# A hybrid attention and state-space layer on one core: joint softmax of two key heads, the scan's state part inside the output's accumulation, and a wider output projection

## The chip, the cores and the metric

The kernel runs on one core of a Trainium2 chip. A core has five engines with instruction queues of their own: TensorE (PE; its weight loads are listed as PEld), VectorE (DVE), ScalarE (ACT), GpSimd (POOL) and SyncE (SP), which here issues all DMAs. Matmuls write PSUM, which has eight banks of 128 partitions by 512 float32; all else lies in SBUF. The metric is the device time of one execution in microseconds, the median of several runs.

## The reference, cut to what matters

One layer is computed for a prompt of 2048 tokens and for a sample group of 8 sequences of 8 tokens. An input projection feeds an attention branch and a state-space branch (SSD), gates weigh both, and an output projection adds the result to the input:

```python
def sink_attention(q, k, v, mask, sinks):            # 16 heads, 4 key heads, window 128
    s = where(mask, einsum(q, k) * HEAD_DIM ** -0.5, -inf)
    m = maximum(s.max(-1), sink);  p = exp(s - m)
    p = p / (p.sum(-1) + exp(sink - m));  return einsum(p, v)

def ssd_scan(x, dt, A, Bm, Cm, h0, chunk):           # 32 heads in 4 groups, chunk 128, state 128
    a_cs = cumsum(dt * A)                            # inside a chunk
    y_diag = einsum(C @ B, exp(a_cs_l - a_cs_s) causal, dt * x)
    states = einsum(Bm, exp(a_cs_end - a_cs) * dt, x)
    h_next = h * exp(a_cs_end) + states              # from chunk to chunk
    y_off  = einsum(Cs, h_prev, exp(a_cs))           # the state's part of the output
    return y_diag + y_off

merged = sigmoid(g_a) * (o_a * silu(z_a)) @ w_attn_proj + sigmoid(g_s) * o_s @ w_ssd_proj
y = x + merged @ w_out                               # 1024 x 1024
```

All inputs and results are float32. The large products split both operands into a high and a low part of a reduced format (`F32R`) and add three products (`SPLIT3`), so a projection over 1024 input channels is 8 x 3 = 24 matmuls.

## The kernel before, in words

The prompt is cut into 4 blocks of 512 tokens, each into 4 tiles (or chunks) of 128. Three phases follow one another. Phase T1 projects and does attention, phase S projects and does the scan, phase T2 does both branch projections, the gates, the merge and the output projection, with the sample group's attention and scan among the first block of T2. The program is written in this order, and a scheduler, which simulates a timeline, sets the order of each engine's queue; there it places attention and scan work among the projections' matmuls. Each queue then runs strictly in its order. Buffers come from pools with a fixed number per tag; who takes one that is still read waits.

**T1, attention.** `attn_unit` handles a pair of key heads and one token tile, 32 units in all. For each key head (four query heads) it makes scores `sc` in PSUM (L541), brings them to `s` (ACT copy L547, masked DVE copy L548), takes the row maximum (L553) and calls `softmax` (L378 to L393): five small DVE operations on 128 x 4, five ACT exponentials, then two of the four heads scaled by ACT (L391) and two by POOL (L393). `s` is then transposed by TensorE (L558), spread into two masked halves `PT` (L560), and when both key heads are there, multiplied with the values (L570).

**S, scan.** For each of 4 groups (8 heads) and 4 chunks, 64 chunks in all, 60 with a state to start from, `AB` is loaded with the cumulated decay of 8 heads on all partitions (L884), `L` is made of it (ACT L887, L888, POOL L889), and `py` is the product of `L` and `dx` (L910): 8 float32 matmuls with 64 stationary columns, which write the upper and the lower half of the partitions in turn. The trace shows every float32 matmul as two passes, each with its own weight load. The state's part is made apart: two DMAs load the decay once more as `EB` (L894), ACT takes its exponential (L895), four matmuls of 128 stationary columns multiply the state `H` with `CT` into `po`, a PSUM bank of its own (L898), and DVE multiplies `po` with `EB` (L899). DVE adds `py` to the skip term `u` (L926), and POOL adds `EB` (L928). `H` is renewed from `st` (L916) by DVE (L923). `py` has one bank.

**T2, output projection.** For each block, four times: 256 channels of `w_o` are loaded (1 MB) and split (ACT L150, DVE L151), and for each of 4 token tiles (in one block a fifth of 64 sample rows) 24 matmuls of 128 x 256 (L210) fill half a PSUM bank. DVE adds the input `xr` into `y` (L1316), which is stored. `xr` and `y` have two buffers each.

Of the kernel before, what the change touches and what calls it, by code (L numbers as in the profile page):

```python
# [17 lines left out]
P = 128  # L18
D = 1024
KT = D // P  # L20
TB = 512
# [57 lines left out]
def build(tc, nc, a, o, seq, phases=("T1", "S", "T2"), dbg=None):  # L79
# [298 lines left out]
    def softmax(wk, s, mx, width, nsk, sk, n):  # L378
        ng = wk.tile([P, 4], F32, name="ng", tag="ng")
        V.scalar_tensor_tensor(out=ng[:, :n], in0=mx[:, :n], scalar=-1.0, in1=nsk, op0=ALU.mult, op1=ALU.min)  # L380
        es_ = wk.tile([P, 4], F32, name="es", tag="es")
        V.tensor_tensor(es_[:, :n], sk, ng[:, :n], ALU.add)
        A.activation(es_[:, :n], es_[:, :n], AF.Exp)
        den = wk.tile([P, 4], F32, name="den", tag="den")
        for i in range(n):
            A.activation(s[:, i, :width], s[:, i, :width], AF.Exp, bias=ng[:, i : i + 1], accum_out=den[:, i : i + 1])  # L386
        V.tensor_tensor(den[:, :n], den[:, :n], es_[:, :n], ALU.add)
        V.tensor_scalar(den[:, :n], den[:, :n], 2.0, None, ALU.mult)
        V.reciprocal(den[:, :n], den[:, :n])  # L389
        for i in range(min(n, 2)):  # L390
            A.activation(s[:, i, :width], s[:, i, :width], AF.Copy, scale=den[:, i : i + 1])  # L391
        for i in range(2, n):
            G.tensor_scalar(s[:, i, :width], s[:, i, :width], den[:, i : i + 1], None, ALU.mult)  # L393

    def phase_t1():
        with ExitStack() as es:
# [12 lines left out]
            sp = pool("sp", 5)  # L409
# [69 lines left out]
            def v_tile(b, hT):  # L479
# [6 lines left out]
                dtt = wk.tile([P, NT, 32], F32, name="dtt", tag="dtt", bufs=1)  # L486
# [40 lines left out]
            def attn_unit(b, pair, tt, qTs, zs):  # L527
# [3 lines left out]
                PTs = []  # L531
                po = trp.tile([P, HG, P], F32, name="tr", tag="tr")
                for kvl in range(2):
                    kv = 2 * pair + kvl
                    s = sp.tile([P, HG, P], F32, name="s", tag="s")
                    mx = smp.tile([P, HG], F32, name="mx", tag="mx")
                    for hh in range(2):
                        sc = scp.tile([P, 2, 256], F32, name="sc", tag="sc")
                        for h in range(2):
                            for i in range(2):  # L540
                                PE.matmul(  # L541
                                    sc[:, h, :W], qTs[kvl][:, 2 * hh + h], KTT[:, i, kv, k0 : k0 + W],
                                    start=i == 0, stop=i == 1,
                                )
                        if full:
                            sv = s[:, 2 * hh : 2 * hh + 2]
                            A.copy(sv, sc[:, :, P:])  # L547
                            V.copy_predicated(sv, older.unsqueeze(1).to_broadcast([P, 2, P]), sc[:, :, :P])  # L548
                        else:
                            for h in range(2):  # L550
                                masked_max(s, mx, 2 * hh + h, sc[:, h, :P], mask, P)
                    if full:
                        V.tensor_reduce(mx, s, AX.X, ALU.max)  # L553
                    softmax(smp, s, mx, P, nsink[:, 4 * kv : 4 * kv + 4], sink[:, 4 * kv : 4 * kv + 4], HG)
                    PT = ptp.tile([P, 2, HG, P], F32, name="PT", tag="PT")
                    tr = trp.tile([P, HG, P], F32, name="tr", tag="tr")
                    for hg in range(HG):
                        PE.transpose(tr[:, hg], s[:, hg], ident)  # L558
# [191 lines left out]
    def phase_s():  # L750
        with ExitStack() as es:
# [14 lines left out]
            yp = pool("y2", 1, space=PSUM)  # L766
            yop = pool("yo2", 1, space=PSUM)
# [99 lines left out]
            def ssd_group(b, g, xT, BT, CT, zs, dt, acs, dec, wd):  # L867
# [11 lines left out]
                for c in range(NT):  # L879
# [47 lines left out]
                    if not first:  # L927
                        G.tensor_tensor(u, u, EB, ALU.add)  # L928
# [246 lines left out]
    def phase_t2():  # L1175
        w_a, w_s, w_o = a["w_attn_proj"][0], a["w_ssd_proj"][0], a["w_out"][0]
        wav = w_a.rearrange("(q v h d) c -> v d q h c", q=2, v=2, h=HG)
        with ExitStack() as es:
# [29 lines left out]

            def wa_load(j):
# [27 lines left out]

            order = [NB - 1] + list(range(NB - 1))
# [9 lines left out]
            for b in order:  # L1248
# [5 lines left out]
                for kh in range(2):  # L1254
# [7 lines left out]
                    if b == order[0] and kh == 1:  # L1262
                        phase_sa(oas)
                        phase_ss(vss)
                    for j in range(4):
# [35 lines left out]
                for j in range(4):  # L1301
                    cs = slice(256 * j, 256 * j + 256)
                    _, hl = wload([(0, w_o[:, cs])])
                    for tt in range(NT + smp):
                        n = P if tt < NT else 64
                        ps = mm()
                        proj_tm(ps[:n, :256], hl, 256, mg, tt, n)
# [5 lines left out]
                        x = wk.tile([P, 256], F32, name="xr", tag="xr")  # L1313
                        SY.dma_start(x[:n], src)
                        y = wk.tile([P, 256], F32, name="y", tag="y")
                        V.tensor_tensor(y[:n], ps[:n, :256], x[:n], ALU.add)  # L1316
                        SY.dma_start(dst, y[:n])
# [47 lines left out]
```

## Time and profile before

| | us |
|---|---|
| median of 3 runs (3144.47 to 3152.12) | 3145.01 |
| the profiled execution | 3143.59 |
| its span, first to last instruction | 3141.8 |
| T1, about 0 to 741 | 741.0 |
| S, about 741 to 1950 | 1209.0 |
| T2 to the last output projection, to 3092 | 1142.0 |
| the last block's output projection, from 3092 | 49.8 |

The phases overlap somewhat at their borders. A row of the profile names a line, an engine, an operation and its tiles as output<-input, then how often it stands there. Busy times of matmuls include their way through the array, which overlaps with the next one's, so that the pace of TensorE is better read from a long piece of the chain divided by its count than from a mean duration. The mean granted clock of TensorE over the span was 0.992.

### The profile page before, as it was taken

To read this page: it belongs to the slowest core of one execution; us is meant where nothing else is said; L and a number is where in the kernel's file an instruction comes from. 1 tells how busy PE (TensorE), PEld (TensorE's weight loads), DVE (VectorE), ACT (ScalarE), POOL (GpSimd) and SP (SyncE) were. 2 spreads that over 40 slices of the span, in tenths; PEclk is the share of its full clock that TensorE was granted. 3 is DMA by queue.
4 is the path that set the end of the run, shared out by engine and by line. 5 is a ranking of instruction groups with operands and counts; after the bars stand their busy time and mean duration, and the time that the engine had idled before them with its cause. 6 is when DMAs were issued, how large, how long until landed. Compare 5 with 4: busy or idle time off the path is not lost.

```text
span 3141.8 us, 49127 instructions
## 1 busy us (share of the span) xinstructions
PE 3059.9 (97%) x18982; PEld 2635.5 (84%) x18982; DVE 1918.5 (61%) x3142; ACT 1356.5 (43%) x2863; POOL 933.1 (30%) x925
## 2 busy tenths in 40 slices
PE   8999999998999999999999998999999999999999
PEld 7979797976999888778877877878878899999888
DVE  5868767677666666676666665456556644333433
ACT  4656545455555444444445453343333322222321
POOL 2425232432455444555554554100111110000000
PEclk9999999999999999999999998999999999999999
DMA  6635345254777755665666564455655663345443
GB/s 223 189 106 148 112 120 166 68 185 154 243 256 259 282 207 202 233 228 188 222 244 212 201 219 142 149 141 172 208 176 144 177 193 123 103 147 159 138 107 104
DMA packets 409986, 553.72 MB, mean 176 GB/s; under 512 B 34145, under 2 KB 347257, under 8 KB 399497
## 3 DMA queue, kind: packets, MB, share of 16 engines
q1 hardware_dynamic: 409752, 550.59, 54.1%
q8 instruction: 149, 2.44, 0.3%
q14 instruction: 85, 0.69, 0.1%
HBM read 445.31 MB, written 107.30 MB: 176 GB/s over the span
## 4 chain that ended last, share of the span: by engine, by line
PE 78%; DVE 8%; DMA 4%; POOL 4%; issue 3%; ACT 2%; SPq 0%; POOLq 0%; DVEq 0%; ACTq 0%
PE mm L199 49%; PE mm L210 13%; PE mm L186 6%; DVE acc L792 2%; PE tr L570 2%; PE sc L541 2%; DVE whl L151 1%; PE py L910 1%; POOL ws L913 1%; POOL L L889 1%; PE tr L558 1%; PE st L916 1%; PE po L898 1%; DMA v<-v_d 1%; DVE zs L929 1%
## 5 line engine op out<-in xcount | busy, mean ns | idle before, releaser
L199 PE MATMUL mm<-hT,whl 128*128 128x512 f32 (+1 forms) x6720 | 1341.4, 355 | 6.1 <-DVE whl L151 3.0
L199 PEld LDWEIGHTS mm<-hT,whl 128*128 128x128 f32 x6720 | 1117.5, 189 | 175.8 <-issue 7.4
L199 PE MATMUL mm<-ot,whl 128*128 128x512 f32 (+1 forms) x2880 | 567.9, 354 | 3.0 <-DVE whl L151 1.4
L199 PEld LDWEIGHTS mm<-ot,whl 128*128 128x128 f32 x2880 | 474.9, 188 | 74.0 <-DVE whl L151 2.9
L151 DVE TENSOR_TENSOR whl<-raw,whl 128x2048 fp32r<-128x2048 f32 (+1 forms) x172 | 366.7, 2137 | 266.5 <-ACT whl L150 259.4
L150 ACT CAST whl<-raw 128x2048 fp32r<-128x2048 f32 (+1 forms) x172 | 298.4, 1746 | 218.0 <-PE mm L199 101.2
L210 PE MATMUL mm<-whl,hT 128*128 128x256 f32 (+1 forms) x2304 | 303.5, 286 | 2.7 <-DVE dtt L491 2.2
L210 PEld LDWEIGHTS mm<-whl,hT 128*128 128x128 f32 x2304 | 286.8, 189 | 7.9 <-issue 4.1
L792 DVE SCALAR_TENSOR_TENSOR acc<-cr,cwb,acc 128x512 f32<-128x512 f32 x288 | 272.5, 948 | 27.3 <-ACT acc L787 24.9
L889 POOL TENSOR_TENSOR L<-L,cbm 128x1024 f32<-128x1024 f32 x64 | 162.2, 2546 | 146.5 <-DVE cbm L878 139.5
L210 PE MATMUL mm<-whl,ot 128*128 128x256 f32 (+1 forms) x1632 | 204.0, 284 | 0.0
L210 PEld LDWEIGHTS mm<-whl,ot 128*128 128x128 f32 (+1 forms) x1632 | 198.8, 188 | 3.7 <-issue 2.1
L186 PE MATMUL mm<-hT,whl 128*128 128x512 f32 x768 | 192.7, 400 | 2.2 <-ACT hT L295 2.1
L887 ACT ACTIVATE L<-AB,acs 128x128 f32<-128x128 f32 x512 | 157.5, 390 | 63.1 <-PE py L910 29.3
L186 PEld LDWEIGHTS mm<-hT,whl 128*128 128x128 f32 x768 | 141.2, 190 | 33.5 <-ACT hT L295 2.5
L859 DVE SCALAR_TENSOR_TENSOR zs<-th,mm 128x512 f32<-128x512 f32 (+1 forms) x80 | 45.6, 577 | 152.4 <-ACT th L858 151.9
L393 POOL TENSOR_SCALAR s<-s,den 128x128 f32<-128x128 f32 x128 | 79.3, 632 | 198.7 <-DVE den L389 144.1
L858 ACT ACTIVATE th<-mm 128x512 f32<-128x512 f32 (+1 forms) x80 | 40.0, 508 | 202.8 <-PE mm L199 196.7
L150 ACT CAST ot<-v 128x512 fp32r<-128x512 f32 x96 | 58.7, 620 | 159.5 <-DVE v L1231 81.0
L386 ACT ACTIVATE s<-s,ng 128x128 f32<-128x128 f32 x256 | 99.9, 394 | 39.9 <-DVE ng L380 32.6
L1231 DVE SCALAR_TENSOR_TENSOR v<-v,snw,rb 128x512 f32<-128x512 f32 x64 | 49.3, 786 | 97.6 <-DMA v<-v_d 97.4
L913 POOL TENSOR_TENSOR ws<-wx,ws 128x512 fp32r<-128x512 f32 x64 | 106.4, 1663 | 5.1 <-ACT ws L912 4.9
(324 smaller groups left out, 3899.6 us busy)
## 6 DMA issues: line engine op xcount, KB each, us to landing
raw<-in_w_in_dram SPq DMA_DIRECT2D x72, 1024.0 KB
whl<-w_dx SPq DMA_DIRECT2D x24, 2048.0 KB
whl<-w_dz SPq DMA_DIRECT2D x24, 2048.0 KB
hT<-h_d SPq DMA_DIRECT2D x80, 512.0 KB
AB<-ac_d SPq DMA_DIRECT2D x64, 512.0 KB
raw<-in_w_ssd_proj_dram SPq DMA_DIRECT2D x32, 1024.0 KB
whl<-w_dbc SPq DMA_DIRECT2D x12, 2048.0 KB
raw<-in_w_in_dram SPq DMA_DIRECT2D x40, 512.0 KB
```

The costliest lines, as they stand in the source:

```text
L150: A.copy(hi, src)
L151: V.tensor_tensor(lo, src, hi.bitcast(F32), ALU.subtract)
L186: PE.matmul(ps, hl[:, x, k, c0 : c0 + P], ht[:, y, :], start=first and i == 0, stop=last and i == n - 1,)
L199: PE.matmul(ps, hl[:, x, k, c0 : c0 + P], ht[:, y, lo : lo + n], start=i == 0, stop=i == 3 * len(hT) - 1,)
L210: PE.matmul(ps, ht[:, x, tt * P : tt * P + m], hl[:, y, k, :n], start=i == 0, stop=i == 3 * len(hT) - 1,)
L386: A.activation(s[:, i, :width], s[:, i, :width], AF.Exp, bias=ng[:, i : i + 1], accum_out=den[:, i : i + 1])
L393: G.tensor_scalar(s[:, i, :width], s[:, i, :width], den[:, i : i + 1], None, ALU.mult)
L541: PE.matmul(sc[:, h, :W], qTs[kvl][:, 2 * hh + h], KTT[:, i, kv, k0 : k0 + W], start=i == 0, stop=i == 1,)
L792: V.scalar_tensor_tensor(out=acc, in0=raw[:, k : k + TB], scalar=cwb[:, k, ct : ct + 1], in1=acc, op0=ALU.mult, op1=ALU.add)
L887: A.activation(L[:, h], AB[:, h], AF.Relu, scale=-1.0, bias=acs[:, hc.start + h : hc.start + h + 1])
L889: G.tensor_tensor(L, L, cbm[:, c].unsqueeze(1).to_broadcast([P, 8, P]), ALU.mult)
L913: G.tensor_tensor(ws[:, 1], wx, ws[:, 0].bitcast(F32), ALU.subtract)
```

## The change

Three edits. Softmax is done once for both key heads of a unit, on 8 columns, after the scores of both; ACT then scales the first key head's four rows, POOL the second's. In the scan, `AB` itself is raised to the exponential after `L` has been made and multiplied by `CT` on DVE, so that the state's part is a second product into the same PSUM tile `py`, which now has two banks; `EB`, its DMAs, `po` and two additions are gone. The output projection takes 512 channels at a time and half of the input channels: four (or five) PSUM banks stay open over both halves.

```diff
     def softmax(wk, s, mx, width, nsk, sk, n):
-        for i in range(min(n, 2)):
+        for i in range((n + 1) // 2):
             A.activation(s[:, i, :width], s[:, i, :width], AF.Copy, scale=den[:, i : i + 1])
-        for i in range(2, n):
+        for i in range((n + 1) // 2, n):
             G.tensor_scalar(s[:, i, :width], s[:, i, :width], den[:, i : i + 1], None, ALU.mult)
...
-            sp = pool("sp", 5)
+            sp = pool("sp", 3)
...
+                s = sp.tile([P, 2 * HG, P], F32, name="s", tag="s")
+                mx = smp.tile([P, 2 * HG], F32, name="mx", tag="mx")
                 for kvl in range(2):
...
-                    if full:
-                        V.tensor_reduce(mx, s, AX.X, ALU.max)
-                    softmax(smp, s, mx, P, nsink[:, 4 * kv : 4 * kv + 4], sink[:, 4 * kv : 4 * kv + 4], HG)
+                if full:
+                    V.tensor_reduce(mx, s, AX.X, ALU.max)
+                heads = slice(2 * HG * pair, 2 * HG * pair + 2 * HG)
+                softmax(smp, s, mx, P, nsink[:, heads], sink[:, heads], 2 * HG)
+                PTs = []
+                for kvl in range(2):
...
-            yp = pool("y2", 1, space=PSUM)
-            yop = pool("yo2", 1, space=PSUM)
+            yp = pool("y2", 2, space=PSUM)
...
                     if not first:
-                        EB = lp.tile([P, 4, P], F32, name="EB", tag="EB")
-                        for hl in range(2):
-                            src = ac_d[b][hc].rearrange("(i l) t -> l i t", l=2)[hl]
-                            SY.dma_start(EB[64 * hl : 64 * hl + 64], src.partition_broadcast(64))
-                        A.activation(EB, EB, AF.Exp)
-                        po = yop.tile([P, 4, P], F32, name="po", tag="po")
-                        for i in range(4):
-                            PE.matmul(po[:, i], H[g][:, i * P : (i + 1) * P], CT[:, sl], start=True, stop=True)
-                        V.tensor_tensor(EB, po, EB, ALU.mult)
+                        A.activation(AB, AB, AF.Exp)
+                        V.tensor_tensor(AB, AB, CT[:, sl].unsqueeze(1).to_broadcast([P, 8, P]), ALU.mult)
...
                     for i in range(4):
-                        for hl in range(2):
-                            PE.matmul(py[64 * hl : 64 * hl + 64, i], dx[:, 2 * i + hl], L[:, 2 * i + hl], start=True, stop=True)
-                    ws = ck.tile([P, 2, 8, 64], F32R, name="ws", tag="ws", bufs=1)
+                        for src, mov in ((dx, L), (H[g].rearrange("p (h d) -> p h d", h=8), AB))[: 1 if first else 2]:
+                            for hl in range(2):
+                                PE.matmul(
+                                    py[64 * hl : 64 * hl + 64, i], src[:, 2 * i + hl], mov[:, 2 * i + hl],
+                                    start=src is dx, stop=first or src is not dx,
+                                )
+                    ws = ck.tile([P, 2, 8, 64], F32R, name="ws", tag="ws")
...
-                    if not first:
-                        G.tensor_tensor(u, u, EB, ALU.add)
...
-                for j in range(4):
-                    cs = slice(256 * j, 256 * j + 256)
-                    _, hl = wload([(0, w_o[:, cs])])
-                    for tt in range(NT + smp):
-                        ps = mm()
-                        proj_tm(ps[:n, :256], hl, 256, mg, tt, n)
+                for j in range(2):
+                    cs = slice(512 * j, 512 * j + 512)
+                    pss = [mm() for tt in range(NT)]
+                    if smp:
+                        pss.append(extra["mm"].tile([P, TB], F32, name="mms", tag="mms")[:64])
+                    for kh in range(2):
+                        hl = wide_load(w_o[512 * kh : 512 * kh + 512, cs])
+                        for tt, ps in enumerate(pss):
+                            for i in range(12):
+                                kk, (x, y) = i // 3, SPLIT3[i % 3]
+                                PE.matmul(
+                                    ps, mg[4 * kh + kk][:, x, tt * P : tt * P + ps.shape[0]], hl[:, y, kk],
+                                    start=kh == 0 and i == 0, stop=kh == 1 and i == 11,
+                                )
...
-                        V.tensor_tensor(y[:n], ps[:n, :256], x[:n], ALU.add)
-                        SY.dma_start(dst, y[:n])
+                        x = wk.tile([P, TB], F32, name="xr", tag="xr")
+                        SY.dma_start(x[:n], src)
+                        V.tensor_tensor(x[:n], ps, x[:n], ALU.add)
+                        SY.dma_start(dst, x[:n])
```

(`wide_load` loads 1 MB as 4 x 128 input channels by 512 output channels and splits it like `wload`. A small tile `dtt` of T1 now shares the buffer of `zt`.)

Three places show how the queues move. The first is TensorE in the scan, two chunks of the last group of a block, as it stood before:

```order
L199 MATMUL mm<-hT,whl 128x512 x8
L910 MATMUL py<-L,dx 64x128 x7
L898 MATMUL po<-CT,H_8560 128x128 x4
L910 MATMUL py<-L,dx 64x128
L916 MATMUL st<-ws,Bt 128x512
L199 MATMUL mm<-hT,whl 128x512 x22
L916 MATMUL st<-ws,Bt 128x512 x2
L199 MATMUL mm<-hT,whl 128x512 x9
L910 MATMUL py<-L,dx 64x128 x8
```
The same place now, where `AB` is the decayed `CT`, `H_8175` the same state as `H_8560`, and L906 and L915 are what L910 and L916 were:

```order
L915 MATMUL st<-ws,Bt 128x512
L906 MATMUL py<-L,dx 64x128 x2
L915 MATMUL st<-ws,Bt 128x512 x2
L897 MATMUL tr<-cst,xT 128x128 x4
L199 MATMUL mm<-hT,whl 128x512 x3
L897 MATMUL tr<-cst,xT 128x128 x4
L199 MATMUL mm<-hT,whl 128x512 x9
L906 MATMUL py<-AB,H_8175 64x128 x2
L906 MATMUL py<-L,dx 64x128 x2
```
The four wide matmuls of the state are gone from between the `py` products. In their place two of 64 columns follow each two of `dx`, on to four such pairs, so every `py` run after the first two matmuls needs the renewed `H`; 97 runs of `py` have become 105, of up to 16 matmuls instead of 8.

The second is ACT at the end of T1, in the last attention units, as it stood before (L386 is an exponential with its sum `den`, L391 the scaling, L547 the copy of scores):

```order
L386 ACTIVATE s,den<-s,ng 128x128 x4
L391 ACTIVATE s<-s,den 128x128 x2
L383 ACTIVATE es<-es 128x4
L391 ACTIVATE s<-s,den 128x128 x2
L386 ACTIVATE s,den<-s,ng 128x128 x4
L547 COPY s<-sc 128x256
L391 ACTIVATE s<-s,den 128x128 x2
L386 ACTIVATE s,den<-s,ng 128x128 x3
L383 ACTIVATE es<-es 128x4
```
The same place now, under the same lines:

```order
L391 ACTIVATE s<-s,den 128x128 x4
L547 COPY s<-sc 128x256 x3
L386 ACTIVATE s,den<-s,ng 128x128 x8
L547 COPY s<-sc 128x256
L383 ACTIVATE es<-es 128x8
L386 ACTIVATE s,den<-s,ng 128x128 x2
L391 ACTIVATE s<-s,den 128x128 x4
L383 ACTIVATE es<-es 128x8
```
Runs of four exponentials with a scaling of two each have become runs of eight with a scaling of four, so the first scaling of a unit stands behind the exponentials of both key heads.

The third is DVE in the last output projection, as it stood before:

```order
L151 TENSOR_TENSOR whl<-raw,whl 128x2048
L1297 SCALAR_TENSOR_TENSOR ot<-ac,ot 128x512
L1316 TENSOR_TENSOR y<-mm,xr 128x256 x4
L151 TENSOR_TENSOR whl<-raw,whl 128x2048
L1316 TENSOR_TENSOR y<-mm,xr 128x256 x4
L151 TENSOR_TENSOR whl<-raw,whl 128x2048
L1316 TENSOR_TENSOR y<-mm,xr 128x256 x8
```
The same place now, where L1331 is the addition of the input, and L1301 and L1304 were L1294 and L1297:

```order
L1301 TENSOR_TENSOR ac<-ac,t 128x512
L151 TENSOR_TENSOR whl<-raw,whl 128x2048
L1304 SCALAR_TENSOR_TENSOR ot<-ac,ot 128x512
L151 TENSOR_TENSOR whl<-raw,whl 128x2048
L1331 TENSOR_TENSOR xr<-mm,xr 128x512 x4
L151 TENSOR_TENSOR whl<-raw,whl 128x2048
L1331 TENSOR_TENSOR xr<-mm,xr 128x512 x4
```
Sixteen additions of 256 channels have become eight of 512, in two groups of four; the last weight split (L151) stands between the groups, behind four additions that each need their input's DMA.

## Rows read from the trace of the kernel before

**Rows 1.** The page, parts 1 and 4: busy time by engine; chain by engine.
```profile
PE 3059.9 (97%) x18982; PEld 2635.5 (84%) x18982; DVE 1918.5 (61%) x3142; ACT 1356.5 (43%) x2863; POOL 933.1 (30%) x925
PE 78%; DVE 8%; DMA 4%; POOL 4%; issue 3%; ACT 2%; SPq 0%; POOLq 0%; DVEq 0%; ACTq 0%
```

**Rows 2.** Four stretches of the program; stretch, its length, busy us (instructions) by engine.
```profile
0.00:741.00 741.00, 698.63 (x4847) 595.78 (x4847) 529.10 (x1105) 399.70 (x1144) 247.54 (x312) 0.99 0.45 142
741.00:1950.00 1209.00, 1181.47 (x6993) 1001.98 (x6991) 817.53 (x1101) 587.62 (x1197) 608.73 (x531) 0.99 0.64 223
2586.00:3092.00 506.00, 505.31 (x3167) 467.23 (x3168) 201.72 (x230) 140.69 (x176) 0.00 (x0) 1.00 0.43 130
3092.00:3141.80 49.80, 46.53 (x387) 46.25 (x385) 15.38 (x22) 6.24 (x4) 0.00 (x0) 1.00 0.32 101
```

**Rows 3.** The chain of waits, longest pieces; start us, length us, what.
```profile
2816.67 57.00 PE mm L210 x480
2907.71 184.75 PE mm L199 x813
3092.46 46.08 PE mm L210 x384
```

**Rows 4.** Groups by line and shape; after the bar: busy us, mean ns.
```profile
L210 PE MATMUL mm<-whl,ot 128*64 128x256 f32 x96 | 11.6, 276 | 0.0
L1294 DVE TENSOR_TENSOR ac<-ac,t 128x512 f32<-128x512 f32 x24 | 16.6, 691 | 0.7
L1316 DVE TENSOR_TENSOR y<-mm,xr 128x256 f32<-128x256 f32 x64 | 26.3, 421 | 75.4 <-PE mm L210 41.1 <-DMA xr<-in_x_prompt_dram 31.4 <-PE st L1129 2.8
```

**Rows 5.** Instructions in order of time, end of the program; start us, length us.
```profile
3113.17 0.42 DVE L1316 TENSOR_TENSOR y<-mm,xr 128x256 f32<-128x256 f32 x1 [2.97 <-DMA xr<-in_x_prompt_dram]
3138.57 0.42 DVE L1316 TENSOR_TENSOR y<-mm,xr 128x256 f32<-128x256 f32 x1 [2.45 <-PE mm L210]
```

**Rows 6.** Groups by line and shape in the scan stage.
```profile
L910 PE MATMUL py<-L,dx 128*64 128x128 f32 x1024 | 81.3, 282 | 5.0 <-DVE xT L926 5.0
L910 PEld LDWEIGHTS py<-L,dx 128*64 128x64 f32 x1024 | 58.0, 137 | 31.1 <-issue 23.9 <-DVE EB L899 1.8 <-DVE zs L929 1.4
L898 PE MATMUL po<-CT,H 128*128 128x128 f32 x480 | 67.3, 284 | 5.0 <-DVE H L923 5.0
L898 PEld LDWEIGHTS po<-CT,H 128*128 128x128 f32 x480 | 60.7, 195 | 11.6 <-DVE H L923 7.1 <-issue 2.6 <-DVE BT L797 0.7
L928 POOL TENSOR_TENSOR xT<-xT,EB 128x512 f32<-128x512 f32 x60 | 87.2, 1454 | 47.6 <-DVE xT L926 27.1 <-DVE EB L899 20.4
L560 DVE TENSOR_TENSOR PT<-tr,halves 128x1024 f32<-128x1024 f32 x60 | 72.3, 1216 | 22.3 <-PE tr L558 22.1
```

**Rows 7.** Instructions in order of time, one chunk of the scan, weight loads.
```profile
1930.15 1.08 PEld L898 LDWEIGHTS po<-CT,H 128*128 128x128 f32 x8
1931.35 0.85 PEld L910 LDWEIGHTS py<-L,dx 128*64 128x64 f32 x16
1932.38 0.19 PEld L916 LDWEIGHTS st<-ws,Bt 128*128 128x128 f32 x1 [0.17 <-issue]
```

**Rows 8.** Waits of TensorE and its weight loads; us in total, times, longest.
```profile
PEld po L898 <- DVE H L923: 7.1, 6, 2.8
PE py L910 <- DVE xT L926: 5.0, 5, 1.3
PE tr L558 <- ACT s L391: 5.0, 3, 2.6
```

**Rows 9.** Groups by line and shape in the softmax.
```profile
L387 DVE TENSOR_TENSOR den<-den,es 128x4 f32<-128x4 f32 x64 | 11.5, 182 | 34.7 <-ACT s L386 34.4
L553 DVE TENSOR_REDUCE mx<-s 128x4 f32<-128x512 f32 x60 | 40.8, 679 | 0.5
L386 ACT ACTIVATE s<-s,ng 128x128 f32<-128x128 f32 x256 | 99.9, 394 | 39.9 <-DVE ng L380 32.6 <-DVE den L389 5.2 <-POOL s L393 1.3
L393 POOL TENSOR_SCALAR s<-s,den 128x128 f32<-128x128 f32 x128 | 79.3, 632 | 198.7 <-DVE den L389 144.1 <-DVE ng L380 19.7 <-DVE es L382 10.9
```

More of the change, by code (lines that the diff above doesn't have):

```diff
@@ L378, in softmax @@
     def softmax(wk, s, mx, width, nsk, sk, n):
-        ng = wk.tile([P, 4], F32, name="ng", tag="ng")
+        ng = wk.tile([P, 8], F32, name="ng", tag="ng")
         V.scalar_tensor_tensor(out=ng[:, :n], in0=mx[:, :n], scalar=-1.0, in1=nsk, op0=ALU.mult, op1=ALU.min)
-        es_ = wk.tile([P, 4], F32, name="es", tag="es")
+        es_ = wk.tile([P, 8], F32, name="es", tag="es")
         V.tensor_tensor(es_[:, :n], sk, ng[:, :n], ALU.add)
         A.activation(es_[:, :n], es_[:, :n], AF.Exp)
-        den = wk.tile([P, 4], F32, name="den", tag="den")
+        den = wk.tile([P, 8], F32, name="den", tag="den")
         for i in range(n):
@@ L485, in v_tile @@
                     G.tensor_copy(vT[:, 0], vT[:, 4])
-                dtt = wk.tile([P, NT, 32], F32, name="dtt", tag="dtt", bufs=1)
+                dtt = wk.tile([P, NT, 32], F32, name="dtt", tag="zt", bufs=1)
                 for tt in range(NT):
@@ L530, in attn_unit @@
                 ws = (0, 1) if full else (1,)
-                PTs = []
                 po = trp.tile([P, HG, P], F32, name="tr", tag="tr")
+                s = sp.tile([P, 2 * HG, P], F32, name="s", tag="s")
+                mx = smp.tile([P, 2 * HG], F32, name="mx", tag="mx")
                 for kvl in range(2):
                     kv = 2 * pair + kvl
-                    s = sp.tile([P, HG, P], F32, name="s", tag="s")
-                    mx = smp.tile([P, HG], F32, name="mx", tag="mx")
                     for hh in range(2):
@@ L544, in attn_unit @@
                                 )
+                        at = HG * kvl + 2 * hh
                         if full:
-                            sv = s[:, 2 * hh : 2 * hh + 2]
+                            sv = s[:, at : at + 2]
                             A.copy(sv, sc[:, :, P:])
@@ L557, in attn_unit @@
                     for hg in range(HG):
-                        PE.transpose(tr[:, hg], s[:, hg], ident)
+                        PE.transpose(tr[:, hg], s[:, HG * kvl + hg], ident)
                     if full:
@@ L1207, in mm, with wide_load @@
                 return mmp.tile([P, TB], F32, name="mm", tag="mm")
+            def wide_load(src):
+                raw, hl = wtile([])
+                raw = raw.rearrange("p k c -> p (k c)").rearrange("p (k c) -> p k c", c=512)
+                hl = hl.rearrange("p i k c -> p i (k c)").rearrange("p i (k c) -> p i k c", c=512)
+                SY.dma_start(raw, src.rearrange("(k p) c -> p k c", p=P))
+                split(hl[:, 0], hl[:, 1], raw)
+                return hl
             def wa_load(j):
@@ L1236, in split_load @@
                 return ot
+            extra = {}
             order = [NB - 1] + list(range(NB - 1))
@@ L1264, in phase_t2 @@
                         phase_ss(vss)
+                        extra["mm"] = pool("mm5", 1, space=PSUM)
                     for j in range(4):
@@ L1300, in phase_t2 @@
                         mg.append(mt)
-                for j in range(4):
-                    cs = slice(256 * j, 256 * j + 256)
-                    _, hl = wload([(0, w_o[:, cs])])
-                    for tt in range(NT + smp):
-                        n = P if tt < NT else 64
-                        ps = mm()
-                        proj_tm(ps[:n, :256], hl, 256, mg, tt, n)
+                for j in range(2):
[12 more added lines that the diff above has]
+                                )
+                    for tt, ps in enumerate(pss):
+                        n = ps.shape[0]
                         if tt < NT:
```

4 lines of the change are left out of this document (1 added, 3 removed).

## The prediction

> **What bounds the kernel now.** I read the page first [rows 1]: TensorE is busy 97% of the span, the next engine, DVE, 61%, and the chain that ended last lies on TensorE for 78%. The reader should see from this that work taken from DVE, ACT, POOL or the DMAs is worth nothing by itself; it counts only where TensorE waited for it. The second view cuts the span into stretches [rows 2]. TensorE is idle for 741.0 - 698.6 = 42.4 us in T1 (the first loads included), for 1209.0 - 1181.5 = 27.5 us in the scan stage S, for 0.7 us in the last 506 us before the last output projection, and 3.3 us in that projection, nearly all of it the tail after the last matmul. So an edit pays in two ways: fewer or cheaper TensorE instructions, or fewer of some 70 us of waits in T1 and S. The third view is the chain, for the pace of matmuls that follow each other without a gap [rows 3].
>
> **The output projection, 512 channels at a time.** Before, 4 blocks x 4 channel groups x 4 tiles x 24 = 1536 matmuls of 128 x 256. The last 384 took 46.08 us [rows 3], 120.0 ns each: 1536 x 0.1200 = 184.3 us. After, half as many with 512 columns; 813 of that width took 184.75 us [rows 3], 227.2 ns each: 768 x 0.2272 = 174.5 us. That is **-9.8 us**. By the other piece (480 in 57.00 us, 118.8 ns [rows 3]) it would be 182.4 - 174.5, so -7.9 us; both ends are near. The 96 matmuls of the sample rows [rows 4] are the rest of that piece, 57.00 - 384 x 0.1200 = 10.9 us, and 48 wide ones at 0.2272 are 10.9 us too: nothing.
>
> Why a column costs less when there are more of them is the fixed part: 120.0 and 227.2 ns are 107.2 ns for 256 further columns and 12.8 ns for each matmul. [...]
>
> The weights are loaded and split in the same four 1 MB pieces per block, each now used for 48 x 0.2272 = 10.9 us where it was 96 x 0.1200 = 11.5 us. DVE and ACT are busy for 15.4 and 6.2 of 49.8 us there [rows 2], so this stays hidden. The four open banks are emptied one by one, 12 x 0.2272 = 2.7 us apart, long before the next channel group returns to them. What is exposed is the end: the last addition grows from 0.42 us [rows 5] to about 0.69 us (a 512-wide addition, L1294 [rows 4]), the last store doubles, and `xr` is now output too, so that a load waits for a store. One such addition already waited 2.97 us for its input [rows 5], under matmuls that went on. I take **+1.0 us**, between +0.3 (the addition alone) and +3 (one more such wait at the very end).
>
> **The scan's TensorE work.** 240 float32 matmuls with 128 stationary columns go (480 passes), 480 with 64 come (960 passes, shaped as the present `py`). The trace has the same shapes [rows 6]. By weight loads, `po` has 60.7 us for 480 and `py` 58.0 us for 1024, so 960 cost 54.4 us: -6.3 us. By matmuls, `po` has 67.3 and `py` 81.3 us, so 960 cost 76.2 us: +8.9 us. I take the middle, **+1.3 us**. One chunk [rows 7] bounds it lower: from the first load of `po` to the first of `py` 1.20 us, while 16 more passes inside `py` would be 0.85 us, its own load time: -0.35 us x 60 = -21 us, if every chunk stood as that one does. Most do not: many `po` stand alone among projections, where there was no switch to save, and 97 runs of `py` become 105.
>
> **The scan's waits.** POOL loses 60 additions (87.2 us [rows 6]), SP 120 DMAs, DVE and ACT swap 512-wide work for 1024-wide: for DVE 1.22 us, by L560 [rows 6], in place of 0.68. These lie beside projections, with DVE at 817.5 of 1209.0 us [rows 2]. TensorE gains the wait for the only `py` bank, 5.0 us [rows 8], since there are two now. A new wait can come: `py` now needs the renewed `H`, as `po` did, for which loads waited 7.1 us in 6 places, 2.8 us at the longest [rows 8]; behind a stalled `py` stand the `st` products and all projection matmuls. `AB` is also held until `py` has read it, so the next but one `AB` load stands in SP's queue later than before, with weight loads behind it. I take **-4 us**; the ends are -24 (nearly all of the 27.5 idle) and +36 (the slow rival).
>
> **The joint softmax.** TensorE's instructions stay. DVE loses 32 x 5 small operations of about 0.18 us [rows 9], 29 us, and some 4 us of reduction (two of 0.68 [rows 9] against one of about 1.22), ACT a little. In return a unit is slower from end to end: eight exponentials of about 0.39 us [rows 9] before the first scaling instead of four, 1.6 us more, and POOL scales four rows in place of two before the second head can be transposed, 2 x 0.63 [rows 9] = 1.3 us more. Transposes waited for scaled rows only 5.0 us in all of T1 [rows 8], so projections cover most of it; at T1's end they don't. I take **-2 us**, less DVE queueing against a longer last unit; the ends are -21 (half of T1's 42.4 idle) and +40 (1.26 us uncovered in each of 32 units).
>
> **Sum.** -9.8 + 1.0 + 1.3 - 4 - 2 = -13.5 us against the profiled execution of 3143.6 us, of which 3141.8 are span and the rest stays: 3130.1 us. The median before is 3145.0, 1.4 us above that execution, too little to move the forecast: **3130 us**, with a range of its own of 3119 to 3137.
>
> **Rivals.**
> - *No change, through the softmax.* The projections cover less than I think: if 10 of 32 units leave their 1.26 us of POOL uncovered, T1 costs 12.6 us more instead of 2 less: 3143.6 - 9.8 + 1.0 + 1.3 - 4 + 12.6 = 3145 us. For it: the scheduler now sets eight transposes in a row more often, and the end of T1 has no cover. Against it: those 5.0 us [rows 8]. Chance 0.22.
> - *A larger gain, in the scan.* Each chunk gains the 0.35 us of the one read [rows 7], in place of +1.3: 3143.6 - 9.8 + 1.0 - 21 - 4 - 2 = 3108 us. For it: fewer changes between matmuls of 128 and of 64 stationary columns. Against it: the +8.9 us by the matmuls' busy time [rows 6]. Chance 0.15.
> - *Slower, through the state.* `py` in one accumulation stalls TensorE until `H` is renewed, at 7.1 / 6 = 1.2 us a time [rows 8]. In 30 of 60 chunks that is +36 us in place of -4: 3143.6 - 9.8 + 1.0 + 1.3 + 36 - 2 = 3170 us. It makes the kernel slower by over 9.4 us from 16 chunks on ((9.4 + 9.5) / 1.2). For it: the state products can't be moved on their own any more. Against it: the scheduler moved them behind the same `H` before, and waited in 6 places. Chance 0.10.
> - *Width is worth nothing.* The 12.8 ns per matmul are a stall that grows with the columns where a token tile is the stationary operand: a wide matmul takes two narrow ones, 240.0 ns, and -9.8 becomes 0: 3130.1 + 9.8 = 3140 us. Against it: 813 traced matmuls at 227.2 ns [rows 3], though with weights as the stationary operand. [...] Chance 0.03.
>
> **How the numbers follow.** The forecast has 0.50. A measurement of this kernel can tell about 0.3%, 9.4 us, from no change: faster is below 3135.6, slower above 3154.4. Faster: 0.46 of the forecast's 0.50, the larger gain's 0.15, 0.02 of the first rival: 0.63. Slower: the state's 0.10. The rest, 0.27, is within. The range is 3106 to 3152: it takes in the first and the last rival and half of the larger gain, and leaves out the slow one.
>
> **What would show it.** Right: L1318 at 227 ns a matmul in a gapless piece, 43.6 us for the last 192; the passes of L906 between 53 and 80 ns; TensorE's idle time in S about 23 us and in T1 about 40. Wrong: weight loads of L906 that wait for `H` in total over 20 us; transposes L561 waiting for POOL; a tail after the last matmul over 6 us; wide matmuls at 240 ns.

## The result and the profile after

The changed kernel takes 3178.05 us (median of 4 runs, 3175.61 to 3184.46) where the kernel before takes 3145.34 (4 runs, 3144.47 to 3152.12): 1.0099 times as long, 95% interval 1.0082 to 1.0116. It is slower, by about 1% and clear of noise; 3130 us and a range of 3106 to 3152 were forecast. The profiled execution took 3178.75 us with a span of 3177.0.

The stretches that answer to [rows 2] show where the time went. First T1 up to the first matmul of the scan stage's projection, which comes at 695.5 us before and at 731.8 after, behind the same 4648 TensorE instructions. Columns: stretch, length, busy us and instructions of PE, PEld, DVE, ACT and POOL, granted clock, DMA share, GB/s. Before:
```profile
0.00:695.50 695.50, 664.06 (x4648) 570.76 (x4648) 497.05 (x1020) 371.43 (x1030) 236.35 (x292) 1.00 0.46 142
```
After, the same stretch, then the stretch of the scan that holds the projection's matmuls 2400 to 4800, then the last 49 us:
```profile
0.00:732.00 732.00, 678.17 (x4648) 580.60 (x4648) 481.89 (x854) 366.60 (x1002) 245.58 (x292) 0.97 0.45 141
1231.60:1938.10 706.50, 705.71 (x4118) 569.09 (x4117) 474.70 (x612) 356.96 (x698) 320.78 (x299) 1.00 0.57 205
3128.00:3177.00 49.00, 43.84 (x194) 35.97 (x192) 14.30 (x14) 6.27 (x4) 0.00 (x0) 0.99 0.28 97
```
The scan's same 2400 matmuls before:
```profile
1186.00:1911.20 725.20, 714.70 (x3799) 578.16 (x3797) 486.89 (x612) 340.06 (x697) 372.62 (x339) 1.00 0.61 214
```
T1 loses 36.3 us: TensorE's idle time grows from 695.5 - 664.1 = 31.4 to 732.0 - 678.2 = 53.8 us, and the same instructions are busy for 14.1 us longer, at a granted clock of 0.97 in place of 1.00. Softmax work did leave the other engines (DVE's busy time fell from 497.05 to 481.89 us), and none of it came back as time. The middle of the scan gains 18.7 us: 9.0 of TensorE's busy time and 9.7 of its idle time (10.5 to 0.8). The span grew by 35.2 us (3141.8 to 3177.0): 36.3 in T1, 9.3 more from there to the start of the scan's stretch (490.5 to 499.8 us; T1's last units run there), -18.7 in the stretch, and 8.3 behind it (1230.6 to 1238.9).

The wide matmuls have the forecast pace. Pieces of the chain of waits after (start, length, what), answering to [rows 3]; 10.88 / 48 and 38.09 / 168 are 226.7 ns:
```profile
2869.62 10.88 PE mm L1318 x48
3128.32 38.09 PE mm L1318 x168
```
The last rival's 240.0 ns for a wide matmul did not come.

TensorE's waits after up to 745 us, the longest but for two at the start (engine, line, for whom: us, times, longest), answering to [rows 8]:
```profile
PE tr L561 <- ACT s L391: 12.8, 2, 9.1
PE tr L573 <- DVE PT L563: 12.0, 8, 2.2
PE sc L540 <- DVE qT L521: 4.6, 3, 2.7
PE tr L449 <- DVE zt L447: 3.6, 1, 3.6
PE tr L561 <- POOL s L393: 2.1, 3, 1.6
```
The prediction's first rival and its sign of being wrong went by the last of these lines, POOL's four rows; it is the smallest of the five. The longest of the first line, 9.08 us, stands in the 28th of T1's 32 units. On TensorE, its first head's scores, the last of its second head's, and its transposes:
```profile
698.56 1.22 PE L540 MATMUL sc<-KTT,qT 128*128 128x256 f32 x8
705.54 0.48 PE L540 MATMUL sc<-KTT,qT 128*128 128x256 f32 x2
720.53 2.51 PE L561 MATMUL tr<-cst,s 128*128 128x128 f32 x8 [9.08 <-ACT s L391]
```
and on ACT and DVE, from the last scores to those transposes:
```profile
705.00 3.70 ACT L150 CAST whl<-raw 128x2048 fp32r<-128x2048 f32 x2
708.00 4.48 DVE L151 TENSOR_TENSOR whl<-raw,whl 128x2048 fp32r<-128x2048 f32 x2
708.90 0.37 ACT L547 COPY s<-sc 128x256 f32<-128x256 f32 x1
713.14 0.43 DVE L548 COPY_PREDICATED s<-cst,sc 128x256 f32<-128x256 int32 x1
714.48 1.21 DVE L553 TENSOR_REDUCE mx<-s 128x8 f32<-128x1024 f32 x1
715.99 0.40 ACT L386 ACTIVATE s<-s,ng 128x128 f32<-128x128 f32 x1 [5.87 <-DVE ng L380]
718.79 0.39 ACT L386 ACTIVATE s<-s,ng 128x128 f32<-128x128 f32 x1
```
The second head's copies stand behind a weight split in both queues (3.70 us on ACT, 4.48 on DVE). The joint maximum cannot start before them, and no exponential of either head before the maximum: 15.0 us from the last scores to the first transpose, and 22 from the first head's scores. In the same unit before, the first head's exponentials began before the last scores, and both heads' had run before the split; the two heads' transposes came 6.4 and 9.6 us after the last scores:
```profile
672.42 0.39 ACT L386 ACTIVATE s<-s,ng 128x128 f32<-128x128 f32 x1
673.68 0.63 PE L541 MATMUL sc<-KTT,qT 128*128 128x256 f32 x4
677.48 0.39 ACT L386 ACTIVATE s<-s,ng 128x128 f32<-128x128 f32 x1
679.06 3.70 ACT L150 CAST whl<-raw 128x2048 fp32r<-128x2048 f32 x2
680.05 0.66 PE L558 MATMUL tr<-cst,s 128*128 128x128 f32 x4
683.26 0.84 PE L558 MATMUL tr<-cst,s 128*128 128x128 f32 x4 [2.56 <-ACT s L391]
688.12 3.68 PE L570 MATMUL tr<-PT,vT 128*64 128x512 f32 x8 [4.01 <-DVE PT L560]
```

### The profile page after: what moved, and what is told of

The parts are those of the page before. It is cut to its first block, busy times and chain, and to the rows that moved or that the text cites. A ratio compares the mean times of both kernels' runs of the same rounds, so it can differ in the third digit from the quotient of the medians.

```text
span 3177.0 us, 47678 instructions
## 1 busy us (share of the span) xinstructions
PE 3059.2 (96%) x18646; PEld 2589.0 (81%) x18646; DVE 1901.1 (60%) x2918; ACT 1375.5 (43%) x2831; POOL 870.8 (27%) x865
## 5 line engine op out<-in xcount | busy, mean ns | idle before, releaser
L151 DVE TENSOR_TENSOR whl<-raw,whl 128x2048 fp32r<-128x2048 f32 (+1 forms) x172 | 365.5, 2129 | 298.0 <-ACT whl L150 297.5
L1318 PE MATMUL mm<-whl,ot 128*128 128x512 f32 x768 | 183.0, 392 | 0.0
L1318 PEld LDWEIGHTS mm<-whl,ot 128*128 128x128 f32 x768 | 142.7, 188 | 31.6 <-issue 2.1
L393 POOL TENSOR_SCALAR s<-s,den 128x128 f32<-128x128 f32 x128 | 86.7, 693 | 207.0 <-DVE den L389 157.0
L386 ACT ACTIVATE s<-s,ng 128x128 f32<-128x128 f32 x256 | 99.3, 391 | 48.3 <-DVE ng L380 43.0
L894 DVE TENSOR_TENSOR AB<-AB,CT 128x1024 f32<-128x1024 f32 x60 | 95.9, 1599 | 20.9 <-ACT AB L893 20.9
L798 ACT ACTIVATE th<-acc 128x512 f32<-128x512 f32 x96 | 60.2, 627 | 110.9 <-DVE acc L794 110.5
```

The source lines that it names most:

```text
L151: V.tensor_tensor(lo, src, hi.bitcast(F32), ALU.subtract)
L894: V.tensor_tensor(AB, AB, CT[:, sl].unsqueeze(1).to_broadcast([P, 8, P]), ALU.mult)
L1318: PE.matmul(ps, mg[4 * kh + kk][:, x, tt * P : tt * P + ps.shape[0]], hl[:, y, kk], start=kh == 0 and i == 0, stop=kh == 1 and i == 11,)
```

## The experiments

Experiments have numbers, and the kernel of experiment 3 is called kernel 3. All compare with the kernel before on the same chip, where it took 3150 to 3152 us, so ratios are compared, not times; 0.1% is 3.2 us. The trace of the kernel before is from a chip where it took 3145 us, so that lengths in traces of two kernels can differ by some 0.2% for that alone.

**1. The softmax alone** (every edit above line 700 of the kernel, on the kernel before; the shared buffer of `dtt` is among them).

> The kernel before with the joint softmax alone (its pools and buffer tags included). Theory: the softmax step, put at -2 us in the prediction, is what failed. In the changed kernel the first matmul of the scan stage's projection came at 731.8 us where it came at 695.5, so this kernel shows the same 36 us in T1 and ends at 3145 + 36 = 3181 us (3172 to 3190). Rival: T1 was late only together with the other edits (another order of the instructions); then this kernel is within 3140 to 3155 us.

Measured: ratio 1.0119 (1.0105 to 1.0132), +37 us. The softmax edit with its shared buffer is the whole loss.

**2. One word.**
```
-dtt = wk.tile([P, NT, 32], F32, name="dtt", tag="dtt", bufs=1)
+dtt = wk.tile([P, NT, 32], F32, name="dtt", tag="zt", bufs=1)
```

> The kernel before with one word changed: the tile dtt of the V projection lies in the buffer of zt, as in the changed kernel. Theory: in block 2 the rows of V can then not leave PSUM until zt is read, so that their matmuls no longer stand between the attention units before them; of the 13 us that the changed kernel loses around 400 to 440 us of its trace some 5 to 10 come from this: 3150 to 3155 us. Rival: the word is worth nothing and all is the softmax's: 3143 to 3147 us.

Measured: 1.0032 (1.0021 to 1.0044), +10 us. Before, three of the V projection's groups (24 matmuls of 288 columns each) stood between the last units of block 1:
```profile
393.39 2.93 PE L210 MATMUL mm<-whl,hT 128*128 128x288 f32 x20 [0.86 <-DVE dtt L491]
398.71 3.46 PE L210 MATMUL mm<-whl,hT 128*128 128x288 f32 x24 [0.98 <-DVE dtt L491]
402.10 1.94 PE L570 MATMUL tr<-PT,vT 128*64 128x512 f32 x8
```
With the one word two of these three, and the fourth group, stand behind the gate's sample columns `zt`, whose buffer `dtt` now has to wait for:
```profile
398.21 3.68 PE L570 MATMUL tr<-PT,vT 128*64 128x512 f32 x8 [1.32 <-DVE PT L560]
405.72 0.45 PE L449 MATMUL tr<-cst,zt 128*128 128x128 f32 x1 [3.42 <-DVE zt L447]
406.68 5.47 PE L210 MATMUL mm<-whl,hT 128*128 128x288 f32 x28
```
The units lose the work that stood beside them, and the 28 matmuls behind the wait take 195 ns each, where 24 took 144. In the changed kernel 27 matmuls in the same place take 222 ns each, at a granted clock of 0.60 (420.40 to 426.40 us), where those 24 had 1.00:
```profile
420.40 6.00 PE L210 MATMUL mm<-whl,hT 128*128 128x288 f32 x27
```

**3. The changed kernel with `dtt` apart** (that word undone; `r2` in one buffer for room).

> The changed kernel with dtt in a buffer of its own again (for room, the temporary r2 of the rows' norm has one buffer in place of two). Theory: gives back what the shared buffer costs and leaves the longer softmax, 3178 - 10 = 3168 us (3165 to 3173). Rival that puts all on the longer softmax: 3176 to 3180 us. Rival that puts all on the shared buffer: 3142 us.

Measured: 1.0062 (1.0049 to 1.0075), against 1.0099: 12 us back, 24 us above kernel 4.

**4. Without the joint softmax** (experiment 1's edits left out).

> The changed kernel without the joint softmax: scan and output projection as changed, T1 as before. Theory: the 36 us of T1 are gone and the rest stays, some 18 us gained in the scan stage and some 12 lost around the first output projection: 3178 - 36 = 3142 us (3136 to 3148). Rival: the scan's gain was only the wait that a late T1 had already served, and goes with it: 3155 to 3160 us.

Measured: 0.9986 (0.9974 to 0.9998). The rest of the change is a small gain. T1, whose code is as before, takes 700.8 us here up to the scan's first matmul where the trace before has 695.5: what a few us there mean can't be told.

**5. Each head normalised by itself again**, in the joint tile with the joint maximum (on kernel 3):
```
-softmax(smp, s, mx, P, nsink[:, heads], sink[:, heads], 2 * HG)
+for kvl in range(2):
+    hs_ = slice(HG * kvl, HG * kvl + HG)
+    hd_ = slice(2 * HG * pair + HG * kvl, 2 * HG * pair + HG * kvl + HG)
+    softmax(smp, s[:, hs_], mx[:, hs_], P, nsink[:, hd_], sink[:, hd_], HG)
```

> The changed kernel with dtt in its own buffer, and each key head normalised by itself again (four exponentials, then its sums, reciprocal and scaling), in the joint tile with the joint row maximum. The kernel with dtt in its own buffer had ratio 1.0062 and its scan stage's projection began at 717.5 us, 22 us later than before. Theory: those 22 us come from the chain of eight exponentials ahead of the first scaling, and most of it goes: 700 us, ratio 1.000 (0.998 to 1.002). Rival: they come from the joint tile and maximum (both heads' scores are awaited before either is worked on, three units in flight), and stay: ratio 1.005 to 1.007.

Measured: 1.0043 (1.0031 to 1.0055). The theory of the eight exponentials fails: 18 of the 24 us stay. The softmax of one head also has two rows scaled by ACT and two by POOL again, so the other 6 need not be the exponentials'.

**6. Scaling shared as before** (on kernel 3: rows 0, 1, 4, 5 on ACT, 2, 3, 6, 7 on POOL).

> The changed kernel with dtt in its own buffer, joint normalisation kept, but the scaling shared as before: two rows of each key head on ACT and two on POOL, where the change gives the first head to ACT and the second to POOL. Theory of the long chain: the first head's rows come no earlier, the last row about as late; ratio 1.004 to 1.007 (1.0062 without it). Rival that blames POOL's four rows of the second head (4 x 0.69 us, my prediction's 1.26 us a unit): some 15 us come back, ratio 1.0015.

Measured: 1.0045 (1.0033 to 1.0057), 5 us below kernel 3, with intervals that overlap. POOL's four rows are not the main cause; whether they cost those 5 us is not resolved.

**7. The order of the transposes alone** (kernel before; one loop over the heads cut in two, before `PT = ptp.tile(...)`).

> The kernel before with one loop cut in two: both key heads' scores and softmaxes first, then both heads' transposes. Tiles, maxima and normalisations stay one per key head. The joint kernel with dtt apart began the scan stage's projection 22 us late, and 17.7 us late with a normalisation per head, so the chain of eight exponentials is not the cause. Theory now: what is late is the order of the code, by which a unit's first transposes stand behind the second head's scores and softmax: ratio 1.003 to 1.006, the scan stage's first projection 10 to 18 us later than before. Rival: it is the joint tile and maximum, by which no row of a unit can be worked on before the scores of all eight heads are there; then this kernel is as before, 0.999 to 1.001.

Measured: 0.9998 (0.9986 to 1.0009). Miss for the theory. But the edit did not reach TensorE: in the trace its 18982 matmul records stand, by the names of their tiles, in the same order as before, since the scheduler sets the order. So this shows only that the order of the code by itself changes nothing; another order of the queue is in kernel 9.

**8. The joint tile alone** (kernel before; `s` and `mx` are slices of one tile, `sp` has 3 buffers).

> The kernel before with the joint tile alone (eight heads' rows in one tile, three of them; r2 in one buffer for room); maximum, softmax and transposes per key head in the order before. By the theory of the code's order it is as before, 0.999 to 1.001; by the rival of the joint tile (a tile is free only when both heads are done, so three units in place of five halves) 1.003 to 1.006.

Measured: 1.0000 (0.9991 to 1.0009). The joint tile costs nothing; here too TensorE's order is as before.

**9 and 10. A maximum per head**, with a normalisation per head (9, on kernel 5) and with the joint one (10, on kernel 3):
```
+        if full:
+            hv = slice(HG * kvl, HG * kvl + HG)
+            V.tensor_reduce(mx[:, hv], s[:, hv], AX.X, ALU.max)
-    if full:
-        V.tensor_reduce(mx, s, AX.X, ALU.max)
```

> The joint kernel with dtt apart, a normalisation per key head and now also a row maximum per key head: joint are only the tile and the order of the code (both heads' scores, then both softmaxes, then both heads' transposes). With the joint maximum it stood at ratio 1.0043. Neither the joint tile alone nor the transposes behind the second softmax alone cost anything. Theory: the joint maximum is what costs, since no exponential can start before the last score of the second head is copied; ratio 0.999 to 1.0015. Rival: the order of the code is, by which the first softmax is issued behind the second head's scores on ACT and DVE anyway: 1.003 to 1.0055.

> The joint kernel with dtt apart and the joint normalisation, but a row maximum per key head. With the joint maximum it stood at ratio 1.0062. Theory: any operation over both heads has the same effect, so this keeps most of the loss: 1.004 to 1.006. Rival: it is the maximum's own place, one long reduction behind the last copy, and the normalisation is worth nothing: 0.999 to 1.002.

Measured: 0.9983 (0.9974 to 0.9992) for 9 and 1.0060 (1.0047 to 1.0074) for 10. 9 lies below its range, which was set against 1.000 by mistake; without any joint softmax the same kernel stands at 0.9986, so all is back, with the joint tile and with another order on TensorE (from 199 us of the trace on). T1 up to the scan's first matmul in kernel 9:
```profile
0.00:700.30 700.30, 667.55 (x4648) 572.17 (x4648) 495.46 (x1020) 370.19 (x1029) 239.83 (x292) 0.99 0.46 141
```
and in kernel 10:
```profile
0.00:728.70 728.70, 675.02 (x4647) 577.84 (x4648) 483.79 (x880) 365.08 (x1001) 243.41 (x292) 0.97 0.46 141
```
TensorE's waits for scaled rows from 107 to 720 us (us, times, longest), in kernel 9 and in kernel 10:
```profile
PE tr L564 <- ACT s L391: 4.1, 2, 3.0
PE tr L562 <- ACT s L391: 8.7, 1, 8.7
```
A joint maximum costs 18 us, a joint normalisation 24, both together 24, neither nothing. Either operation over both heads is enough: it makes the first head's rows wait for the second head's. Kernel 10 also has the first head's rows scaled by ACT and the second's by POOL; how much of its 24 us that is (some 5 in experiment 6, not resolved) no run separates.

**11. The scan's change alone.**

> The scan's change alone. The prediction put it at -2.7 us (TensorE's work +1.3, waits -4), its rival at -25. The kernel without the joint softmax gained 20 us between 1059 and 1902 us of its trace and had lost 5 at T1's end, 6 at the scan's start and lost 8 at its end. If these belong to the scan's change the kernel is at 0.998 to 0.9995; if they come from the projection's side, 0.992 to 0.995.

Measured: 0.9965 (0.9954 to 0.9977), -11 us; the first range holds it.

**12. Additions in halves.** The output projection loses in total what the scan gains beyond kernel 4: 0.9986 - 0.9965 = +0.21%, +7 us, where -8.8 was forecast (the two intervals just touch). On kernel 4, each bank added in two halves of 256 channels, `xr` and `y` apart.

> The changed kernel with T1 as before; the wide projection stays, but each bank is added and stored in two halves of 256 channels, xr and y in buffers of their own, as before. It asks what the 13 us are that the kernel without the joint softmax loses beside the first output projection (2553 to 2605 us of its trace against 2559 to 2598 before). Theory: an xr that is also the output must wait for its store, SP stands there 10.7 us in 6 places, the sample stage's state loads behind it come late, and with them the next block's inputs; so some 10 us come back: ratio to before 0.9955 (0.994 to 0.997), where the kernel without the joint softmax had 0.9986. Rival: the loss is the width's (all banks come free at once, in lumps of 24 matmuls), and nothing comes back: 0.998 to 1.000.

Measured: 0.9974 (0.9963 to 0.9985), between theory and rival, and not apart from kernel 4's.

**13 to 15. Where the projection is wide** (on kernel 12): in all blocks but the first of T2 (13), in the last two only (14), in the first two only (15); the other blocks have the old code. 14's condition is `b in order[:2]`, 15's `b in order[2:]`.
```
+if b == order[0]:
+    for j in range(4):
...
+    continue
```

> As the kernel before this one (T1 as before, halves of 256 channels added with xr and y apart), but the first block's output projection is the old one, 256 channels at a time; the other three blocks are wide. Both theories: the first block is as before, so the 13 us come back less the 2.4 us that the width gains in that block: ratio 0.995 (0.993 to 0.997). If it is no better than 0.998, the loss is not the output projection's at all but comes from the scan's new order.

> T1 as before, the scan as changed, the output projection wide in the last two blocks only, with its additions in halves. Theory: the wide projection loses where it stands beside the sample stage's state updates (first two blocks), which end at 2578 us of the trace in place of 2553, and the third block's inputs wait for their end. With the two blocks narrow they end as before, within 5 us, nothing is lost at the third block and two blocks' 4.9 us of width are kept: ratio 0.995 (0.993 to 0.997). Rival: what the third block loses comes with the scan's new order; then 0.997 to 0.999.

> The complement of the kernel that was wide in the last two blocks only (ratio 0.9959; the scan alone 0.9965): wide in the first two blocks, beside the sample stage, and narrow in the last two. Theory: the width's loss lies here, some 8 us net beside the scan alone: 0.998 to 1.000. Rival: width gains the same 2.4 us in every block: 0.995 to 0.997.

Measured: 13 0.9974 (0.9965 to 0.9983), outside its range; 14 0.9959 (0.9947 to 0.9971), inside; 15 0.9980 (0.9970 to 0.9990), at the edge of its theory's. Beside the sample stage the width brings +0.15% over the scan alone; behind it -0.06%. Neither is resolved by itself: both intervals overlap that of the scan alone, and those of 14 and 15 touch.

Kernel 14 is the fastest found, 13 us below the kernel before; its gain over the scan alone is not resolved. What the trace shows of the first two blocks: the sample stage's state updates fill the same waits with more time. Between two of them stand 33 narrow matmuls before, 4.1 us,
```profile
2207.22 0.39 PE L1130 MATMUL st<-Bel,wxs 128*128 128x512 f32 x1
2207.44 4.10 PE L210 MATMUL mm<-whl,ot 128*128 128x256 f32 x33
2211.38 0.39 PE L1129 MATMUL st<-Beh,wxs 128*128 128x512 f32 x1
```
and 23 wide ones in kernel 12, 5.4 us:
```profile
2212.31 0.40 PE L1124 MATMUL st<-Bel,wxs 128*128 128x512 f32 x1
2212.54 5.41 PE L1315 MATMUL mm<-whl,ot 128*128 128x512 f32 x23
2217.79 0.39 PE L1123 MATMUL st<-Beh,wxs 128*128 128x512 f32 x1
```
The stage's last store goes out at 2552.79 us before
```profile
2552.79 0.50 SPq L1167 DMA_DIRECT2D rss_d<-r  x1
```
and 58.6 us later in the changed kernel, 22 more than T1's delay; the third block needs its result and waits 6.82 us (in kernel 14 the store goes out at 2552.66 us, and this wait is gone):
```profile
2611.37 0.49 SPq L1164 DMA_DIRECT2D rss_d<-r  x1
```
TensorE there, the third block's matmuls of the SSD part:
```profile
2603.85 8.60 PE L199 MATMUL mm<-ot,whl 128*128 128x288 f32 x64
2619.27 20.89 PE L199 MATMUL mm<-ot,whl 128*128 128x288 f32 x141 [6.82 <-ACT ot L150]
```

**16. The sample rows in the last block** (kernel 12, `order[min(3, NB - 1)]` in place of 2), so that nobody waits for the stage.

> Scan and output projection as changed, T1 as before, additions in halves (the kernel at ratio 0.9974), with one number changed: the sample rows go with the last block of T2 in place of the third. Theory: the wide projection makes the sample stage end some 25 us late, and that costs only since the third block waits for it; with the sample rows in the last block nothing waits and the projection's gain shows: ratio 0.994 to 0.9965. Rival: the loss is in the first two blocks' own work (additions, weights, stores beside the state updates): 0.9970 to 0.9985.

Measured: 0.9980 (0.9970 to 0.9990). Miss: the wait is real, but to take it away gives nothing back. What the width loses in these two blocks stays open; the spacing of the state updates is a reading, not shown.

## Why the prediction was wrong

- **The joint softmax, -2 us: the step that failed.** It measured +24 us without the shared buffer (kernel 3 against kernel 4) and +12 more with it. The step counted 2.9 us of longer chain and held it covered, since transposes had waited only 5.0 us for scaled rows [rows 8]. That was one link of the chain: at the next one, `PT`, TensorE already waited 14.4 us before (us, times, longest):
```profile
PE tr L570 <- DVE PT L560: 14.4, 8, 4.0
```
And a cover that was just enough for two half units in turn says nothing of one whole unit: before, the first head's exponentials could run ahead of the second head's copies, and a joint operation ends that (experiments 5, 9 and 10). In the unit shown the chain grew by what stood in the queues of ACT and DVE before the second head's copies, a weight split, from 6.4 to 15.0 us behind the last scores, and not by 2.9; that the other units lost their time in the same way is not shown. The rows of that unit show it on ACT: scores that end at 706.02 us, and their copy of 0.37 us at 708.90, behind casts that take 3.70 from 705.00 on.
- **The tag of `dtt`, priced at nothing and not named.** +10 us alone, 12 in the changed kernel: the V projection's matmuls were the cover of the units beside them.
- **The clock.** Neither term had it. Of T1's 36.3 us, 14.1 are the same instructions at a lower granted clock (0.97, before 1.00). Where TensorE was idle for half of 20 us, the granted clock was 0.70, and 0.87 in the next 20 us without a gap (before, both stretches had 1.00):
```profile
400.00:420.00 20.00, 10.23 (x36) 5.11 (x37) 7.61 (x16) 6.08 (x27) 4.69 (x8) 0.70 0.13 39
420.00:440.00 20.00, 20.00 (x179) 19.59 (x178) 4.50 (x12) 3.67 (x8) 1.84 (x3) 0.87 0.22 66
```
These runs show no fixed price. In kernel 3, up to the same matmul, 18.3 us more of idle time came with 3.7 us more of busy time, at a granted clock of 0.98:
```profile
0.00:717.50 717.50, 667.73 (x4648) 571.96 (x4648) 480.57 (x854) 365.92 (x1002) 246.04 (x292) 0.98 0.47 144
```
- **The scan, +1.3 and -4: the sum's sign right, its size too small, the first term's sign wrong.** -11 us alone (-7 to -15). In the stretch shown, 40 chunks gain 18.7 us, or 0.47 each, half of it busy time: TensorE's work fell by 9.0 us there, where +1.3 was reckoned for all 60. The price by matmuls, +8.9 us, was the wrong one of the two: 20 passes of L906 from 1972.76 us on take 1.09 us, 54.5 ns each, near the 57 ns of the weight loads [rows 6] and not the 79 of the matmuls. The read chunk's 0.35 us [rows 7] was the better guide. The rival of the larger gain was still wrong: the scan alone brings 11 of its 25 us, some being given back outside that stretch, and without the softmax the kernel stands at 0.9986 (kernel 4), some 3141 us and not 3108. Whether fewer changes between shapes make the gain, no run separates. The slow rival's wait did come, for `H` behind L906, but small (us, times, longest, from 780 to 1995 us):
```profile
PE py L906 <- DVE H L922: 6.7, 2, 4.5
```
- **The projection, -9.8: right in its matmuls, wrong in its sum.** The last block's 192 take 43.7 us where 384 took 46.1, as forecast:
```profile
3128.16 43.68 PE L1318 MATMUL mm<-whl,ot 128*128 128x512 f32 x192
```
Over all blocks the edit costs some 7 us beside the scan's (kernel 4 against kernel 11). Kernels 14 and 15 point at the first two blocks, beside the sample stage, as the place where it is given back; by what, stays open.
- **Its tail, +1.0:** from the last matmul's end to the span's end 3177.0 - 3171.8 = 5.2 us, before 3141.8 - 3138.5 = 3.3, so +1.9. The last load waits for a store, as feared, under the last matmuls and beyond (two pieces of the chain, then the last addition):
```profile
3167.16 3.05 DMA out_dram<-xr
3170.22 2.94 DMA xr<-in_x_prompt_dram
3173.29 0.69 DVE L1331 TENSOR_TENSOR xr<-mm,xr 128x512 f32<-128x512 f32 x1 [2.96 <-DMA xr<-in_x_prompt_dram]
```
- Of what would show it wrong, only the weakest sign was named for T1 (waits for POOL, 2.1 us); the right one, T1's idle time over 40 us, stood among the signs of being right. It was meant for T1 up to 741 us, 4847 instructions; nearly as many (4841) end at 780 us after, and 780.0 - 712.2 = 67.8 us of it are idle:
```profile
0.00:780.00 780.00, 712.18 (x4841) 604.24 (x4843) 511.29 (x915) 393.57 (x1111) 256.50 (x311) 0.96 0.43 134
```

## What to carry to other kernels

Before two independent chains are joined by one operation, ask what the one does while the other waits: the saving is in instructions, the price in the overlap that ends. Price a shared buffer by who is released later, and what work stood in that place as cover. And look at the granted clock behind a new gap on TensorE: in the changed kernel it was 0.87 from 420 to 440 us, without a gap there, behind 20 us that were half idle; in the same 20 us of the kernel before it was 1.00.

## What was not expected of the hardware

How much busy time came with gaps and a lower granted clock: 22.4 us more of idle time in T1 came with 14.1 us more of busy time for the same 4648 instructions at 0.97 in place of 1.00, but in kernel 3 18.3 us with 3.7 at 0.98.
